# A residual attention block on one core: where the low parts of the column tiles' weights are made

## Chip, core and metric

The kernel runs on one core of a Trainium2 chip. The metric is the device time of one execution in microseconds. Three runs of the kernel before took 858.71, 859.07 and 860.24 us; their median is 859.07 us.

## What is computed

One layer on 512 tokens of width 2048, in float32: an RMS norm, one input projection that is cut into queries, keys, values and gates of eight stick-breaking heads and into the latents and gates of eight latent-attention heads, both attentions, an output projection, a second norm and the residual.

```python
h = rms_norm(x, pre_norm_w)
proj = h @ w_in
sb_q, sb_k, sb_v, sb_gate, c_q, c_kv, k_rope, mla_gate = jnp.split(proj, split_pts, axis=-1)
o_a = from_heads(stick_breaking_attention(to_heads(sb_q, SB_HEADS), to_heads(sb_k, SB_HEADS), to_heads(sb_v, SB_HEADS)))
...
o_b = from_heads(chunk_causal_softmax_attention(q_mla, k_mla, v_mla.transpose(0, 2, 1, 3)))
mixed = jnp.concatenate([o_a * jax.nn.silu(sb_gate), o_b * jax.nn.silu(mla_gate)], axis=-1)
y = mixed @ w_out
return x + rms_norm(y, post_norm_w)
```

## The kernel before

**Two parts of a number.** TensorE multiplies values of a shorter float type (float32r). Each float32 operand is therefore held as a high part, the value rounded to that type, and a low part, the value less its high part. A product of two operands is three matmuls that add up in one PSUM bank (`mm3`): high by high, high by low, low by high.

**Weights.** `weights` (line 104) brings a piece of 128 x 1024 float32, 512 KB, and splits it. SyncE's queue (SP) loads it into a `raw` tile, of which there are two. ScalarE (ACT) casts it to the high part `whi` (line 96), then VectorE (DVE) subtracts to get the low part `wlo` (line 99). There are three `whi` and three `wlo` tiles, so the parts of one piece can be made once TensorE (PE) has finished with the piece three places earlier.

```python
i = act.copy(out=hi, in_=src)
dve.tensor_tensor(out=lo, in0=src, in1=hi.bitcast(F32), op=ALU.subtract)
```

**Column tiles.** `column_proj` (line 217) makes 128 columns of the input projection, transposed, for all tokens. One column tile takes two pieces of `w_t`, and each piece serves 8 products of three 128x512 matmuls. In a product the matmul that reads `wlo` comes last. There are 32 column tiles, 64 pieces: the gates of the eight latent heads (PSUM tile `gps`), and a query (`qp`), a key (`kp`) and a gate (`gps`) tile for each stick-breaking head. The pieces of the other projections (`cq`, `ckv`, `v`) and of the output (`y`) come through `weights` as well, in the same three-tile ring.

**Order of the work.** PE runs its matmuls in the order in which the program states them. A generator (`filler`, line 449) holds everything that isn't attention: `ckv`, the latent heads' gates, then for every fourth head four heads' values, and for each head query, key and gate, and last the output projection. Attention code calls `fill(n)` to put n of these products between its own steps, so that PE has something to do while ACT and DVE work on scores. The other engines' orders come from a scheduler. Each engine runs its own list strictly in order, and an instruction that waits holds up those behind it.

**GpSimd's queue (POOL)** is touched too. It issues the loads of the latent heads' small weights (`mraw`, line 114), it clears two small tiles for each head (`th` and `tl`, lines 588 and 589), it puts each head's result `mix` aside in memory (`mixed`, line 607) and brings it back for the output projection (`mx`, line 392). A load of `mraw` waits for DVE to be done with the load before it, a store of `mix` for DVE's product, and a load of `mx` for DVE's split of an earlier one.

**Attention.** In a latent head ACT takes the exponentials `p` of the scores `mz` (line 662), after loading its table of functions. PE's next scores wait for `p` where both buffers of scores are taken. In a stick-breaking head ACT computes `keep` and `beta` (lines 745 and 746).

Of the kernel before, what the change touches and what calls it, by code (L numbers as in the profile page):

```python
# [10 lines left out]
F32 = mybir.dt.float32  # L11
F32R = mybir.dt.float32r
# [7 lines left out]
P = 128  # L20
# [12 lines left out]

# slots of [128, 512] float32 by kind, and pieces of the weights in flight
SLOTS = {"g": 46, "q4": 4, "row": 6, "tr": 4, "t": 4, "gt": 2, "mv": 4, "qrt": 8}
# [5 lines left out]
def _bits(v, n):  # L41
    """v cut to n significant bits."""
    m, e = math.frexp(v)
    return math.ldexp(float(round(math.ldexp(m, n))), e - n)
# [13 lines left out]
def block(ctx: ExitStack, tc: tile.TileContext, a: dict):  # L58
# [28 lines left out]
    def load(out, in_):  # L87
        tc.keep_in_program_order(nc.sync.dma_start(out=out, in_=in_))
# [3 lines left out]

# [1 line left out]
    def split(hi, lo, src, scale=None, pin=False):  # L94
# [9 lines left out]
    def weights(src, n):  # L104
# [5 lines left out]
        return hi, lo  # L110

    def small_weights(src, n, pin=False):
        raw = ring.tile([P, 768], F32, tag="mraw", name="mraw", bufs=1)
        pool.dma_start(out=raw[:, :n], in_=src)
        hi = ring.tile([P, 768], F32R, tag="mhi", name="mhi", bufs=1)
        lo = ring.tile([P, 768], F32R, tag="mlo", name="mlo", bufs=1)
        split(hi[:, :n], lo[:, :n], raw[:, :n], pin=pin)
        return hi, lo

    # TensorE runs what is traced, in that order: the order below keeps it fed.  # L120
    def mm(out, lhsT, rhs, start, stop, **kw):
# [9 lines left out]

# [1 line left out]
    pre_w = const.tile([P, NK], F32, name="pre_w")  # L133
# [18 lines left out]
    def rms_factor(name, ss, n, cols):  # L152
        """(ss / n + eps) ** -0.5"""
        m = tn(name + "_m", cols)
        dve.tensor_scalar(out=m, in0=ss, scalar1=1.0 / n, scalar2=EPS, op0=ALU.mult, op1=ALU.add)
        r = const.tile([P, cols], F32, name=name)
        pool.tensor_tensor(out=r, in0=m, in1=mhalf[:, :cols], op=ALU.pow)
        return r

    # TensorE's clock rises while it works  # L160
    idle = g("idle", BF16)
# [4 lines left out]

# [1 line left out]
    hh, hl = [], []  # L168
# [20 lines left out]
    def group_proj(src, width, banks, first=False):  # L189
        """Token-major projection of all blocks of tokens, chunk by chunk; yields after each product."""  # L190
        cuts = [(0, 1), (1, 2)] if first else [(0, 2)]
        cuts += [(k, k + 2) for k in range(2, NK, 2)]
        for k0, k1 in cuts:
            parts = []
            if first:
                # the first chunk of x comes in halves, the weights between them
                parts = [load_h(k, (slice(0, 256), slice(256, S)) if k == 0 else (slice(0, S),)) for k in range(k0, k1)]
                for p_ in parts:
                    next(p_)
            i, o = k0 // 2, (k0 % 2) * width  # L200
            wh, wl = weights(src[i, :, o:o + (k1 - k0) * width], (k1 - k0) * width)
            for p_ in parts:
                next(p_, None)
            for k in range(k0, k1):
                c = slice((k - k0) * width, (k - k0 + 1) * width)
                if first and k == 0:
                    for st, mv in ((hh, wh), (hl, wh), (hh, wl)):
                        for b in range(NB):
                            mm(banks[b][:, :width], tokens(st[k], b), mv[:, c], st is hh and mv is wh, False)
                    continue  # L210
                for b in range(NB):
                    mm3(banks[b][:, :width], tokens(hh[k], b), tokens(hl[k], b), wh[:, c], wl[:, c], k == 0, k == NK - 1)
                    yield
            if first and k0 >= 4:
                square_x(3)

    def column_proj(t, out):
        """One tile of 128 columns, transposed: [column, token]; yields after each product."""
        for half in range(2):
            wh, wl = weights(a["w_t"][t, half], 1024)  # L220
            for j in range(8):
                k = half * 8 + j
                c = slice(j * P, (j + 1) * P)
                mm3(out, wh[:, c], wl[:, c], hh[k], hl[k], k == 0, k == NK - 1)
                yield

# [1 line left out]
    cq_banks = [zbank("cq") for _ in range(2)] + [tbank("cq") for _ in range(2)]  # L228
    for _ in group_proj(a["w_cq"], 512, cq_banks, first=True):
        pass  # L230

# [1 line left out]
    pos_i = tiny.tile([P, NB], I32, tag="tinyi", name="pos_i", bufs=1)  # L233
# [18 lines left out]
    def turns(n, unit, name):  # L252
        """fraction of a turn in n * unit radians, n a whole number of at most 12 bits"""
        c1, c2, c3 = _parts(math.fmod(unit / TWO_PI, 1.0), (12, 12))
        t = sm(name)
        dve.tensor_scalar(out=t, in0=n, scalar1=c1, scalar2=None, op0=ALU.mult)
        w = rounded(t, 1.0, name + "w")
        dve.tensor_tensor(out=t, in0=t, in1=w, op=ALU.subtract)
        fma(t, n, c2, t)
        fma(t, n, c3, t)  # L260
        return t
# [25 lines left out]

    # [block, half, 32]: cosines twice; sines with the sign of their half; the queries' ones scaled
    tabs = {}
# [22 lines left out]
    def latent(banks, n, width, name):  # L312
        """The scaled projection, token-major, and the sums of squares of its first n columns."""
        ssl = const.tile([P, NB], F32, name=name + "ss")
        cs = []
        for b in range(NB):
            c = g(f"{name}{b}")
            dve.tensor_scalar(out=c[:, :width], in0=banks[b][:, :width], scalar1=rstd[:, b:b + 1], scalar2=None, op0=ALU.mult)
            junk = g("junk", tag="tr")
            act.activation(out=junk[:, :n], in_=c[:, :n], func=AF.Square, accum_out=ssl[:, b:b + 1])  # L320
            cs.append(c)
        return cs, ssl
# [12 lines left out]

# [1 line left out]
    done = {}  # L337

    def gate(t, name):
        """silu of a tile of gate columns, transposed."""  # L340
        ps = bank("gps")
        yield from column_proj(t, ps)
        gr = g(name, tag="gt")
        dve.tensor_tensor(out=gr, in0=ps, in1=rstd_bc, op=ALU.mult)
        sg = g("sg", tag="tr")
        act.activation(out=sg, in_=gr, func=AF.Sigmoid)
        dve.tensor_tensor(out=gr, in0=gr, in1=sg, op=ALU.mult)
        return gr
# [26 lines left out]

    # chunks of the output projection: the latent heads' first
    order = list(range(H, 2 * H)) + list(range(H))
# [43 lines left out]
    def resident_weights():  # L421
        """The next two chunks of the last columns' weights."""
        raw = ring.tile([P, 1024], F32, tag="raw", name="raw", bufs=N_RAW)
# [53 lines left out]
    def rotary_queries(grp, new_bank):  # L477
# [10 lines left out]
        ps = [new_bank("qrp") for _ in range(2)]  # L488
        # the two blocks of a bank are one accumulation, which the first of its products starts
        for c in range(4):  # L490
# [23 lines left out]
    def rotary_turn(stacks):  # L514
        """[high; low] of four heads' rotary queries, transposed."""
        out = []
# [9 lines left out]

# [1 line left out]
    cqs, ssq = latent(cq_banks, 512, 512, "cq")  # L528
# [13 lines left out]

    # rstd of every token along the free axis, on every partition
    rb_ps = zbank("rb_ps")
# [8 lines left out]

# [1 line left out]
    ct, st = tabs["k"]  # L555
# [13 lines left out]

# [1 line left out]
    def row_tiles(name):  # L571
        """The rows of the four blocks of queries, the short ones beside each other."""
        t0, t1, t2 = (g(name, tag="row") for _ in range(3))
        return [t0[:, 384:], t1[:, :256], t0[:, :384], t2]

    class Weighted:
        """(sum over s of vals[s, :]^T rows[q, s]) * gate, transposed, by blocks of keys."""

# [29 lines left out]

# [1 line left out]
    def mla_values(pair):  # L610
# [13 lines left out]
    class Latent:  # L624
        """Scores and softmax of a latent head."""

# [58 lines left out]
    for h in range(H + 1):  # L685
# [39 lines left out]
        if h < H and h % 2 == 0:  # L725
            fill(2)
            vals[h // 2] = mla_values(h // 2)
            fill(2)
        # a head's worth of gate columns for every head
        fill(max(0, 4 * NK + NK * (h + 2) - taken[0]))  # L730

# [1 line left out]
    for h in range(H):  # L733
# [27 lines left out]

# [1 line left out]
    for _ in steps:  # L763
# [94 lines left out]
```

## Time and profile before

| what | value |
|---|---|
| median of three runs | 859.07 us (858.71 to 860.24) |
| profiled execution, first to last instruction (span) | 857.2 us |
| own time of the profiled execution | not recorded beside its span; the median is 1.9 us above the span |
| PE busy | 844.1 us, 98% of the span |
| DVE busy | 425.0 us, 50% |
| ACT busy | 337.8 us, 39% |
| POOL busy | 42.1 us, 5% |
| bytes moved by DMA | 97.19 MB, a mean of 113 GB/s |

The busy time of an engine is the sum of its instructions. Matmuls are pipelined and their ends are modelled, so one is shown as 389 ns long while the next starts 227 ns after it. The chain of waits follows the span back from its last instruction, at each step to what released it. PE is named on 93% of it.

### The profile page before, as it was taken

To read this page: it belongs to the slowest core of one execution; us is meant where nothing else is said; L and a number is where in the kernel's file an instruction comes from. 1 tells how busy PE (TensorE), PEld (TensorE's weight loads), DVE (VectorE), ACT (ScalarE), POOL (GpSimd) and SP (SyncE) were. 2 spreads that over 40 slices of the span, in tenths; PEclk is the share of its full clock that TensorE was granted. 3 is DMA by queue.
4 is the path that set the end of the run, shared out by engine and by line. 5 is a ranking of instruction groups with operands and counts; after the bars stand their busy time and mean duration, and the time that the engine had idled before them with its cause. 6 is when DMAs were issued, how large, how long until landed. Compare 5 with 4: busy or idle time off the path is not lost.

```text
span 857.2 us, 10780 instructions
## 1 busy us (share of the span) xinstructions
PE 844.1 (98%) x4146; PEld 711.9 (83%) x4146; DVE 425.0 (50%) x757; ACT 337.8 (39%) x585; POOL 42.1 (5%) x100
## 2 busy tenths in 40 slices
PE   8999999999999999999999999999999999999995
PEld 5889988888888888888888888888888888888885
DVE  5576755556556433536354524446364623244333
ACT  6743655554454423424243314323243423134201
POOL 1010000000000110000000000000001000000001
PEclk9999999999999999999999999999999999999998
DMA  9823222222221252222222224222223232336364
GB/s 314 317 75 101 99 86 75 81 93 80 93 81 62 76 192 97 79 100 85 97 88 86 89 96 135 99 86 95 89 81 132 97 110 99 111 103 204 112 190 153
DMA packets 32627, 97.19 MB, mean 113 GB/s; under 512 B 4144, under 2 KB 4672, under 8 KB 32576
## 3 DMA queue, kind: packets, MB, share of 16 engines
q1 hardware_dynamic: 27792, 82.46, 28.5%
q0 software_dynamic: 3488, 12.08, 4.3%
q10 hardware_dynamic: 1296, 1.97, 0.7%
q8 instruction: 32, 0.52, 0.3%
q14 instruction: 19, 0.16, 0.1%
HBM read 88.37 MB, written 8.13 MB: 113 GB/s over the span
## 4 chain that ended last, share of the span: by engine, by line
PE 93%; DVE 3%; ACT 1%; DMA 1%; issue 0%; POOL 0%; DVEq 0%; SPq 0%; ACTq 0%; POOLq 0%
PE y L122 20%; PE gps L122 19%; PE qp L122 10%; PE v L122 10%; PE kp L122 10%; PE cq L122 4%; PE av L122 4%; PE mz L122 3%; PE mqp L122 3%; PE ckv L122 2%; PE tp L125 2%; PE z L122 2%; PE qrp L122 1%; PE mv L122 1%; PE mkp L122 1%; DMA raw<-in_w_cq 1%
## 5 line engine op out<-in xcount | busy, mean ns | idle before, releaser
L99 DVE TENSOR_TENSOR wlo<-raw,whi 128x1024 fp32r<-128x1024 f32 (+2 forms) x124 | 147.5, 1190 | 187.8 <-ACT whi L96 186.0
L96 ACT CAST whi<-raw 128x1024 fp32r<-128x1024 f32 (+2 forms) x124 | 127.0, 1024 | 251.5 <-PE y L122 58.4
L122 PE MATMUL gps<-hh,whi 128*128 128x512 f32 x256 | 102.0, 398 | 0.0
L122 PE MATMUL gps<-hl,whi 128*128 128x512 f32 x256 | 100.1, 391 | 0.0
L122 PE MATMUL gps<-hh,wlo 128*128 128x512 f32 x256 | 99.9, 390 | 0.0
L122 PE MATMUL y<-whi,mxh 128*128 128x512 f32 (+1 forms) x222 | 85.5, 385 | 0.0
L122 PE MATMUL y<-whi,mxl 128*128 128x512 f32 (+1 forms) x222 | 85.1, 383 | 0.0
L122 PE MATMUL y<-wlo,mxh 128*128 128x512 f32 (+1 forms) x222 | 85.1, 383 | 0.0
L122 PEld LDWEIGHTS gps<-hh,wlo 128*128 128x128 f32 x256 | 48.1, 188 | 10.6
L122 PEld LDWEIGHTS gps<-hl,whi 128*128 128x128 f32 x256 | 48.2, 188 | 7.6
L122 PEld LDWEIGHTS gps<-hh,whi 128*128 128x128 f32 x256 | 48.2, 188 | 7.5
L122 PE MATMUL qp<-hh,whi 128*128 128x512 f32 x128 | 52.0, 407 | 0.0
L96 ACT CAST th<-tp 128x512 fp32r<-128x512 f32 (+1 forms) x64 | 27.1, 423 | 63.2 <-PE tp L125 63.2
L99 DVE TENSOR_TENSOR tl<-tp,th 128x512 fp32r<-128x512 f32 (+1 forms) x64 | 31.2, 488 | 39.9 <-ACT th L96 39.5
L122 PE MATMUL v<-whi,hh 128*128 128x512 f32 x128 | 50.9, 397 | 0.0
L122 PE MATMUL qp<-hh,wlo 128*128 128x512 f32 x128 | 50.1, 391 | 0.0
L122 PE MATMUL qp<-hl,whi 128*128 128x512 f32 x128 | 50.0, 391 | 0.0
L122 PE MATMUL v<-whi,hl 128*128 128x512 f32 x128 | 49.9, 390 | 0.0
L122 PE MATMUL v<-wlo,hh 128*128 128x512 f32 x128 | 49.9, 390 | 0.0
L122 PE MATMUL kp<-hh,whi 128*128 128x512 f32 x128 | 49.8, 389 | 0.0
L122 PE MATMUL kp<-hl,whi 128*128 128x512 f32 x128 | 49.8, 389 | 0.0
L122 PE MATMUL kp<-hh,wlo 128*128 128x512 f32 x128 | 49.8, 389 | 0.0
(246 smaller groups left out, 1618.5 us busy)
## 6 DMA issues: line engine op xcount, KB each, us to landing
raw<-in_w_t SPq DMA_DIRECT2D x64, 512.0 KB, 3.2
raw<-in_w_o SPq DMA_DIRECT2D x32, 512.0 KB, 3.2
raw<-in_w_v SPq DMA_DIRECT2D x16, 512.0 KB, 3.2
xs<-in_x SPq DMA_DIRECT2D x16, 256.0 KB, 6.2
xr<-in_x SPq DMA_DIRECT2D x16, 256.0 KB, 4.9
xt<-in_xt SPq DMA_DIRECT2D x15, 256.0 KB, 5.7
mixed<-mix POOLq DMA_DIRECT2D x15, 256.0 KB, 2.3
mx<-mixed POOLq DMA_DIRECT2D x15, 256.0 KB, 3.4
```

What stands on the lines that cost most here:

```text
L96: i = act.copy(out=hi, in_=src)
L99: dve.tensor_tensor(out=lo, in0=src, in1=hi.bitcast(F32), op=ALU.subtract)
L122: tc.keep_in_program_order(pe.matmul(out=out, lhsT=lhsT, rhs=rhs, start=start, stop=stop, **kw))
L125: tc.keep_in_program_order(pe.transpose(out, in_, identity))
```

## The change

`column_proj` takes its pieces from a new function. ACT now writes the negated high part into `wlo`: it multiplies by -1 and rounds to float32r in one instruction. A DMA on POOL's queue then reads the same piece of the weights from memory a second time and adds it onto `wlo` in place. ACT makes `whi` with a second instruction. DVE no longer takes part in these 64 pieces. All other pieces go through `weights` as before.

```diff
+    def weights_by_dma(src, n):
+
+        raw = ring.tile([P, 1024], F32, tag="raw", name="raw", bufs=N_RAW)
+        load(out=raw[:, :n], in_=src)
+        hi = ring.tile([P, 1024], F32R, tag="whi", name="whi", bufs=N_HI)
+        lo = ring.tile([P, 1024], F32R, tag="wlo", name="wlo", bufs=N_HI)
+        act.activation(out=lo[:, :n], in_=raw[:, :n], func=AF.Copy, scale=-1.0)
+        pool.dma_start(out=lo[:, :n], in_=src, accum_op=ALU.add)
+        act.copy(out=hi[:, :n], in_=raw[:, :n])
+        return hi, lo
+
...
     def column_proj(t, out):
...
         for half in range(2):
-            wh, wl = weights(a["w_t"][t, half], 1024)
+            wh, wl = weights_by_dma(a["w_t"][t, half], 1024)
             for j in range(8):
```

The orders of PE and of SP stay as they were. Those of ACT, DVE and POOL are the scheduler's, and they change at many places. In the kernel of the change line numbers are 11 higher from `small_weights` on; line 118 is the negation, 119 the accumulating DMA and 120 the cast.

The first place is ACT in the first latent head, between the split of its keys (`mkh`) and its exponentials (`p`). Before:

```order
91 L96 CAST mkh<-mkp 128x512
92 L96 CAST whi<-raw 128x1024
93 L346 ACT_TABLE_LOAD
94 L346 ACTIVATE sg<-mg 128x512
95 L662 ACT_TABLE_LOAD
96 L662 ACTIVATE p,sm<-mz,nm 128x128
```

And now:

```order
96 L96 CAST mkh<-mkp 128x512
97 L120 CAST whi<-raw 128x1024
98 L118 ACTIVATE wlo<-raw 128x1024
99 L357 ACT_TABLE_LOAD
100 L357 ACTIVATE sg<-mg 128x512
101 L673 ACT_TABLE_LOAD
102 L673 ACTIVATE p,sm<-mz,nm 128x128
```

One instruction, the negation, stands in front of the gate's sigmoid `sg` and of the first exponential.

The second place is ACT where the fifth stick-breaking head begins, around the split of its queries (`qh`). Before:

```order
324 L96 CAST mxh_5969<-mx 128x512
325 L96 CAST mxh_6005<-mx 128x512
326 L96 CAST whi<-raw 128x1024 x2
327 L96 CAST qh<-qp 128x512
328 L96 CAST whi<-raw 128x1024 x2
```

And now:

```order
376 L96 CAST mxh_6033<-mx 128x512
377 L96 CAST mxh_6069<-mx 128x512
378 L120 CAST whi<-raw 128x1024
379 L118 ACTIVATE wlo<-raw 128x1024
380 L120 CAST whi<-raw 128x1024
381 L96 CAST qh<-qp 128x512
382 L118 ACTIVATE wlo<-raw 128x1024
383 L120 CAST whi<-raw 128x1024
384 L118 ACTIVATE wlo<-raw 128x1024
```

Each cast has a negation behind it, and one of the negations stands behind the split of the queries too.

The third place is POOL from the end of the fourth stick-breaking head to the end of the fifth. Before:

```order
72 L588 MEMSET th 128x128
73 L589 MEMSET tl 128x128
74 L607 DMA mixed_1217<-mix 128x512
75 L392 DMA mx<-mixed_1214 128x512
76 L392 DMA mx<-mixed_1215 128x512
77 L392 DMA mx<-mixed_1216 128x512
78 L588 MEMSET th 128x128
79 L589 MEMSET tl 128x128
80 L607 DMA mixed_1218<-mix 128x512
```

And now:

```order
90 L599 MEMSET th 128x128
91 L600 MEMSET tl 128x128
92 L618 DMA mixed_1218<-mix 128x512
93 L119 DMA wlo<-in_w_t 128x1024 x3
94 L403 DMA mx<-mixed_1215 128x512
95 L403 DMA mx<-mixed_1216 128x512
96 L403 DMA mx<-mixed_1217 128x512
97 L119 DMA wlo<-in_w_t 128x1024 x7
98 L599 MEMSET th 128x128
99 L600 MEMSET tl 128x128
100 L618 DMA mixed_1219<-mix 128x512
```

Ten accumulating DMAs have come between POOL's own work, three of them ahead of the loads of `mx` and seven behind them.

## Rows read from the trace of the kernel before

**Rows 1.** The page: busy time by engine, and the chain of waits by engine.
```profile
PE 844.1 (98%) x4146; PEld 711.9 (83%) x4146; DVE 425.0 (50%) x757; ACT 337.8 (39%) x585; POOL 42.1 (5%) x100
...
PE 93%; DVE 3%; ACT 1%; DMA 1%; issue 0%; POOL 0%; DVEq 0%; SPq 0%; ACTq 0%; POOLq 0%
```

**Rows 2.** Busy us by stretch: length, PE, PEld, DVE, ACT, POOL; clock, DMA, GB/s.
```profile
98.00:270.00 172.00, 171.31 (x897) 146.34 (x896) 104.25 (x243) 91.02 (x177) 13.00 (x30) 1.00 0.24 81
270.00:522.00 252.00, 252.00 (x1179) 210.19 (x1178) 114.72 (x170) 87.80 (x134) 10.06 (x26) 1.00 0.29 99
522.00:670.00 148.00, 148.00 (x692) 123.66 (x691) 78.14 (x117) 56.63 (x93) 6.70 (x16) 1.00 0.31 104
```

**Rows 3.** Waits of PE: for whom, us in total, times, longest.
```profile
PE cq L122 <- DVE wlo L99: 1.0, 2, 0.8
PE mz L122 <- ACT p L662: 0.7, 1, 0.7
...
PE av L122 <- DVE tl L99: 0.2, 1, 0.2
```

**Rows 4.** Groups by shape: count, busy us, mean ns, idle before and its releasers.
```profile
L99 DVE TENSOR_TENSOR wlo<-raw,whi 128x1024 fp32r<-128x1024 f32 x114 | 139.6, 1224 | 181.4 <-ACT whi L96 179.6 <-PE av L122 1.1
```

**Rows 5.** Timeline of ACT, the second place of the change: start, length, instruction.
```profile
532.72 1.05 ACT L96 CAST whi<-raw 128x1024 fp32r<-128x1024 f32 x1 [4.38 <-PE qp L122]
533.67 0.58 ACT L96 CAST qh<-qp 128x512 fp32r<-128x512 f32 x1
```

**Rows 6.** Timeline of PE: first matmul on `wlo` of two pieces.
```profile
533.20 0.39 PE L122 MATMUL kp<-hh,wlo 128*128 128x512 f32 x1
...
544.08 0.39 PE L122 MATMUL gps<-hh,wlo 128*128 128x512 f32 x1
```

**Rows 7.** Timeline of ACT at the casts of the first two column pieces.
```profile
88.78 1.05 ACT L96 CAST whi<-raw 128x1024 fp32r<-128x1024 f32 x1
...
93.02 1.05 ACT L96 CAST whi<-raw 128x1024 fp32r<-128x1024 f32 x1 [0.36 <-PE ckv L122]
93.97 1.17 ACT L522 CAST qrt<-qtp 128x512 fp32r<-128x512 f32 x2
```

**Rows 8.** Timeline of PE: first matmul on the first column piece's `wlo`.
```profile
98.41 0.39 PE L122 MATMUL gps<-hh,wlo 128*128 128x512 f32 x1
```

**Rows 9.** DMA issues: KB each, median us from issue to landing.
```profile
raw<-in_w_t SPq DMA_DIRECT2D x64, 512.0 KB, 3.2
...
mraw<-in_w_head POOLq DMA_DIRECT2D x8, 384.0 KB, 3.3
...
mraw<-in_w_kvv POOLq DMA_DIRECT2D x4, 256.0 KB, 2.8
```

**Rows 10.** DMA queue of SP: packets, MB, share of 16 engines' span.
```profile
q1 hardware_dynamic: 27792, 82.46, 28.5%
```

**Rows 11.** Timeline of ACT and PE, the first place of the change.
```profile
114.54 1.05 ACT L96 CAST whi<-raw 128x1024 fp32r<-128x1024 f32 x1 [2.29 <-PE gps L122]
...
118.85 0.37 ACT L662 ACTIVATE p<-mz,nm 128x128 f32<-128x128 f32 x1
...
119.36 0.44 PE L122 MATMUL mz<-mkh,mqh 128*128 128x384 f32 x1 [0.69 <-ACT p L662]
```

**Rows 12.** Timeline of POOL at four places.
```profile
112.78 0.55 POOL L114 DMA_DIRECT2D mraw<-in_w_head  x1 [5.72 <-DVE mlo L99]
132.46 0.55 POOL L114 DMA_DIRECT2D mraw<-in_w_head  x1 [19.13 <-DVE mlo L99]
...
451.93 0.54 POOL L607 DMA_DIRECT2D mixed<-mix  x1 [5.88 <-DVE mix L603]
...
525.93 1.75 POOL L392 DMA_DIRECT2D mx<-mixed  x3 [35.69 <-DVE mxl L99]
```

**Rows 13.** Busy us in one stick-breaking head, columns as in rows 2.
```profile
365.20:403.00 37.80, 37.80 (x179) 31.60 (x178) 18.59 (x28) 13.15 (x21) 0.95 (x3) 1.00 0.27 91
```

## Prediction

> **What bounds the kernel now.** I began with the page. PE is busy for 844.1 of 857.2 us and is named on 93% of the chain, while DVE is busy for half of the span, ACT for 39% and POOL for 5% [rows 1]. So an instruction that leaves DVE is worth only what PE waits for it. Column tiles run from 98 to 670 us, and the table of stretches gives PE 171.31 of 172 us, 252 of 252 and 148 of 148, at a granted clock of 1.00 (the 2.4 GHz level) [rows 2]. All that could be won there is 0.69 us. PE's waits say what it is: 0.7 us for the exponentials `p` of ACT, once, and 0.2 us for `tl`. The 1.0 us that PE waits for a `wlo` belongs to the tile `cq`, at the start, which the change leaves alone [rows 3]. DVE does stand idle for 179.6 us until a cast ends [rows 4], but nobody on the path waits for DVE. The question is therefore not what DVE gains, but whether the new way of making `wlo` stays inside the time that the old one had to spare.
>
> **DVE's part.** Removed are 64 subtractions of 1.224 us [rows 4], 78 us of DVE's 425. Their cover is PE's work, so I count 0. At most they give back 0.69 us, all the idle time that there is.
>
> **ACT's part.** Added are 64 negations. The nearest row is the cast of the same shape, 1.05 us [rows 5]: 67 us, which lifts ACT from 338 to about 405 of 857 us, so the engine doesn't become the bound. What counts is who stands behind a negation. In the first latent head it lies between the cast at 114.54 and the exponential at 118.85, for which PE already waits 0.69 us, until 119.36 [rows 11]. There is no cover left, so the whole delay goes to the end. An instruction behind such a cast starts 0.95 us after it (93.02 to 93.97 [rows 7]), so this costs **+0.95 us**. Elsewhere PE waits for no work of ACT between 98 and 670 us, and I take 0. The other end is 0.95 us in each of the seven other latent heads, 6.7 us.
>
> **SP's part.** SP's list is the same. A `raw` tile used to be free 1.05 + 1.22 us after its cast began, when the subtraction ended; now it is free after two ACT instructions, 0.95 + 1.05 us. The loads come no later: 0.
>
> **POOL's part.** Added are 64 issues of about 0.55 us [rows 12], 35 us on an engine with 42 busy. They queue in order with waiting instructions. Where the fifth stick-breaking head begins, three loads of `mx` wait until 525.93 and take 1.75 us, so POOL is free at 527.7 [rows 12]. The fourth accumulation stands behind them. The casts come one piece apart, 5.44 us (PE's first `wlo` matmuls at 533.20 and 544.08 are two pieces apart [rows 6]), so its cast begins at about 532.72 - 5.44 = 527.28 [rows 5], its negation ends 2.0 us later, and it finds POOL free with 1.6 us to spare. After a head's store of `mix` (0.54 us at 451.93) POOL is free at once. I count 0, and a hold counts like a longer landing (first rival).
>
> **The accumulation itself.** This operation isn't in the trace, so I set its landing against the time that it has. That time is shortest at the second place of the change. There the cast starts at 532.72, the split `qh` ends at 534.25 [rows 5], the negation would end at about 535.2, and PE wants this `wlo` at 544.08 [rows 6]: **8.9 us**. The first column piece is a second tight spot: its cast ends at 89.83 [rows 7] and PE reads its `wlo` at 98.41 [rows 8], 8.6 us, or 7.6 us if the negation stands behind the cast.
>
> The landing can't be shorter than that of a plain load. POOL's loads land after 2.8 us for 256 KB and 3.3 us for 384 KB [rows 9], so 512 KB need about 3.8 us: the low end. How much is data? SP's queue spent 28.5% of 857.2 us on 82.46 MB [rows 10], 2.96 us for a MB, so a piece of 0.524 MB keeps all engines busy for 1.55 us. An accumulation also has to read its destination. If this doubles the data's part, it lands after 3.8 + 1.55 = **5.4 us**. The high end is reading the weights, reading the destination and writing it one after another, each as long as a load: 3 x 3.8 = 11.4 us. I take 5.4 us, since the row nearest to it is POOL's load, with the same issue and the same bytes from memory. This is under 7.6 us, so it costs 0.
>
> The Trainium skill has a rule on the doubling (Collectives: The Full Stack, "The bandwidth ceiling: the fold count and why AG ≠ RS ≠ AR"): the add in the DMA engine costs nothing by itself, but the two reads halve an engine's rate, from about 31 to 16 GB/s. By that, an estimate, 32 KB on each of 16 engines take 2.0 us where the rows give 3.1, and the sum stays as it is. No row here shows an accumulation.
>
> POOL's loads, with DVE busy half the time, land about as fast as SP's 512 KB in 3.2 us [rows 9], so I see no hindrance of POOL's transfers by DVE. The Trainium skill names one that speaks against this change (SBUF — State Buffer, "A bandwidth-pool intuition that's wrong"): a transfer issued by POOL took about 3.1 in place of 0.62 us beside a DVE copy, because its descriptors had to wait. By that rule the landing would be about 5.4 + 2.5 = 7.9 us, an estimate, still inside 8.9 us but not always inside the first piece's 7.6, and the sum would be 0 to 0.3 us higher.
>
> **Traffic.** For each piece the DMA engines would be busy 1.55 us for the load and 3.1 us for the accumulation, 4.65 us. A piece is due every 5.44 us at the densest and every 37.8 / 6 = 6.3 us over a stick-breaking head [rows 13]. It fits.
>
> **Sum.** 857.2 + 0.95 = 858.2 us for the span. The median of the runs stands 1.9 us above this execution's span, so I forecast **860.0 us**, 0.1% more. A measurement of this kernel can tell about 0.2% (1.7 us) from no change; this would mostly be read as the same.
>
> **Rivals.**
> 1. *A wait of PE on the accumulation* (slower). Place: the third matmul of a product on a new piece, at the first column piece and once in each of the eight stick-breaking heads, where the room is smallest. It decides from a landing, holds on POOL included, of some 7.6 us at the first and 8.9 us at the others. From there each further us costs about 9 us in all. At the high end, 11.4 us, it is 3.8 + 8 x 2.5 = 24 us: 884. For it: nothing in the trace bounds the read of the destination, and POOL's queue holds for up to 19.13 us in the latent heads [rows 12]. Against it: 5.4 us leaves more than 2 us.
> 2. *The DMA engines become the bound* (much slower). This decides where the accumulation keeps them busy for over 6.3 - 1.55 = 4.75 us a piece, three times a plain load. At six times, 9.3 us, 48 pieces lack 10.85 - 6.3 = 4.55 us each, 218 us: 1078. Against it: DMA is busy 24 to 31% in these stretches [rows 2], and double reading adds only 3.1 us to a piece.
> 3. *ACT's extra instruction is paid in every latent head* (slower): 6.7 us more, 866.7. Against it: a single wait for `p` in the trace.
> 4. *Faster*: the lists of ACT and DVE fall so that the one wait doesn't grow and the 0.69 us go: 856.5 for the span, 858.4, still within 0.2%. More than that PE hasn't got to give in these stretches.
>
> **How the numbers follow.** The forecast has a chance of 0.60, rival 1 0.20, rival 2 0.10, rival 3 0.08, rival 4 0.02. Of the forecast 0.52 lies within 0.2%, 0.07 above (some more ACT delays) and 0.01 below. Of rival 1, 0.18 is over 0.2% slower and 0.02 within; rival 2 is slower; rival 3 gives 0.07 slower and 0.01 within; rival 4 splits evenly. Together: faster 0.02, same 0.56, slower 0.42. The range runs from rival 4's 858.4, less 0.2 for the spread of the runs, to rival 1 at its high end, 884, and 1 us for the term of ACT's bound: 858.2 to 885. It leaves out rival 2 and some of the edges.
>
> **What would show it.** In the profile after: a DMA row `wlo<-in_w_t` x64 with a median landing of some 5 to 6 us; DVE near 347 us and ACT near 405 us busy; PE's wait for `p` up from 0.7 to about 1.6 us; no wait of PE for `wlo` between 98 and 670 us. Landings over 9 us with PE waiting on `wlo` in each head are rival 1, a DMA share near 1 there is rival 2, seven waits for `p` are rival 3. I am wrong if PE loses more than 2 us between 98 and 670 us.

## The result, and the profile after

The changed kernel takes **864.43 us** (863.61 to 864.50), the kernel before 859.07: 1.0058 times as long, interval 1.0038 to 1.0078. That is 5.4 us more. It lies inside the range, but it is not the 860.0 of the forecast, and it is not within the 0.2% that the prediction calls the same.

The page of the kernel after, busy time and chain, stands against [rows 1]:

```profile
PE 845.3 (98%) x4146; PEld 712.7 (83%) x4146; DVE 351.9 (41%) x693; ACT 395.7 (46%) x649; POOL 96.0 (11%) x164
...
PE 87%; issue 3%; DMA 3%; ACT 2%; DVE 2%; POOL 1%; DVEq 0%; SPq 0%; ACTq 0%; POOLq 0%
```

DVE lost 73 us and ACT gained 58; the forecast was 78 and 67. What is new is that DMA, ACT, DVE and "issue" hold 10% of the chain; before it was 5%. The stretches, with the columns of [rows 2], tell where:

```profile
98.00:270.00 172.00, 169.17 (x879) 143.78 (x878) 86.90 (x226) 101.98 (x190) 25.18 (x44) 1.00 0.52 129
270.00:522.00 252.00, 252.00 (x1184) 210.40 (x1183) 84.83 (x144) 110.89 (x159) 31.46 (x52) 1.00 0.62 148
522.00:670.00 148.00, 148.00 (x691) 123.63 (x691) 51.26 (x90) 76.43 (x112) 25.96 (x39) 1.00 0.81 185
```

The latent heads, 98 to 270 us, lose 2.1 us of PE's busy time against [rows 2]. The stick-breaking heads lose nothing, though the DMA engines are 2.1 to 2.6 times as busy as before, and the granted clock is 1.00 everywhere. PE's waits, against [rows 3], name two waits that grew, and neither is for `wlo`:

```profile
PE mz L133 <- ACT p L673: 1.6, 1, 1.6
PE av L133 <- DVE tl L99: 1.5, 3, 0.7
```

PE executes the same 4146 matmuls in the same order in both traces, so the start of each can be subtracted from its start before. The shift is 0.15 us at 98 us. It jumps by 0.95 us at the matmul of [rows 11] (119.36 before, now 120.47), by 0.74 us at two near 189 us, by 1.24 us at three near 235 us and by 0.32 us between 672 and 675 us. At the last matmul it is 3.46 us. The span grew by 5.6 us (862.8 for 857.2), so 2.1 us more are lost *after* the last matmul. There the work is the same; what differs is the last DRAIN of POOL and of SP. The source view of the program's last line, before and then after; the columns are shortest, median and longest ns, then the first and last start in us:

```profile
L854 POOLq DRAIN  x3: 40/102/5619, 850.5 to 856.9; - x3
L854 SPq DRAIN  x3: 7/7/7, 856.4 to 856.7; - x3
```

```profile
L865 POOLq DRAIN  x3: 46/102/7982, 854.0 to 862.5; - x3
L865 SPq DRAIN  x3: 7/7/7, 859.8 to 862.2; - x3
```

POOL's longest drain started at 850.55 and took 5.62 us: done at 856.2, just under SP's first drain at 856.4. Now it starts at 854.0, takes 7.98 us and ends at 862.0, when SP has been ready since 859.9. These are the 2.1 us.

The DMA issues and the queues of the kernel after, against [rows 9, 10]:

```profile
raw<-in_w_t SPq DMA_DIRECT2D x64, 512.0 KB, 4.4
wlo<-in_w_t POOLq DMA_DIRECT2D x64, 512.0 KB, 7.7
```

```profile
q1 hardware_dynamic: 27792, 82.46, 29.7%
q0 software_dynamic: 12704, 45.64, 26.8%
```

An accumulation lands after 7.7 us, not 5.4, and SP's loads beside it became slower (4.4 for 3.2 us). PE still never waits for one: over all tiles from 98 us on the longest landing is 8.5 us.

Where do the shifts at 189 and 235 us come from? The chain of waits of the kernel after, in order of time (start, us, what), at the first of them:

```profile
181.19 0.54 POOL wlo L119
181.73 7.00 DMA mraw<-in_w_head
188.72 0.02 issue
188.75 0.02 ACTq L96
188.76 0.04 issue
188.80 0.84 ACT mhi L96
189.65 0.02 issue
189.67 0.41 DVE mlo L99
190.08 0.47 issue
190.55 0.56 DVE tl L99
191.11 0.04 issue
191.15 0.62 PE av L133 x2
```

Read it upwards. PE waits for `tl`; DVE made it late because `mlo` stood ahead of it; `mlo` waited for ACT's `mhi`; and `mhi` waited for the small weights `mraw`, whose load POOL issued right behind an accumulation. The load took 7.0 us. Its median before was 3.3 [rows 9]. Nobody needs these small weights yet, but ACT and DVE work in order, and the rows of the softmax queue behind them.

The 0.3 us between 672 and 675 us have a cause of the same kind. The chain there starts with the first of four loads of `mx`, which POOL issues next after its last accumulation. It lands after 4.1 us; in the kernel before it landed after 2.9. This was read off the traces and not tried by itself.

### The profile page after: what moved, and what is told of

Its sections match the earlier page's. It is cut to its first block, busy times and chain, and to the rows that moved or that the text cites. A ratio compares the mean times of both kernels' runs of the same rounds, so it can differ in the third digit from the quotient of the medians.

```text
span 862.8 us, 10897 instructions
## 1 busy us (share of the span) xinstructions
PE 845.3 (98%) x4146; PEld 712.7 (83%) x4146; DVE 351.9 (41%) x693; ACT 395.7 (46%) x649; POOL 96.0 (11%) x164
## 4 chain that ended last, share of the span: by engine, by line
PE 87%; issue 3%; DMA 3%; ACT 2%; DVE 2%; POOL 1%; DVEq 0%; SPq 0%; ACTq 0%; POOLq 0%
PE y L133 20%; PE gps L133 16%; PE qp L133 10%; PE v L133 10%; PE kp L133 10%; PE cq L133 4%; PE av L133 3%; PE mz L133 2%; PE ckv L133 2%; PE mqp L133 2%; PE tp L136 2%; DMA mraw<-in_w_head 2%; PE z L133 2%; PE qrp L133 1%; DMA raw<-in_w_cq 1%
## 5 line engine op out<-in xcount | busy, mean ns | idle before, releaser
L96 ACT CAST whi<-raw 128x1024 fp32r<-128x1024 f32 (+2 forms) x60 | 59.6, 993 | 129.7 <-PE y L133 57.1
L99 DVE TENSOR_TENSOR wlo<-raw,whi 128x1024 fp32r<-128x1024 f32 (+2 forms) x60 | 69.2, 1154 | 105.7 <-ACT whi L96 105.5
L120 ACT CAST whi<-raw 128x1024 fp32r<-128x1024 f32 x64 | 67.1, 1048 | 88.1 <-issue 38.9
L119 POOL DMA_DIRECT2D wlo<-in_w_t x64 | 54.7, 854 | 342.5 <-ACT wlo L118 292.1
L118 ACT ACTIVATE wlo<-raw 128x1024 fp32r<-128x1024 f32 x64 | 67.6, 1056 | 15.3 <-PE v L133 14.9
```

The lines of the kernel that those rows point to most:

```text
L118: act.activation(out=lo[:, :n], in_=raw[:, :n], func=AF.Copy, scale=-1.0)
L119: pool.dma_start(out=lo[:, :n], in_=src, accum_op=ALU.add)
L120: act.copy(out=hi[:, :n], in_=raw[:, :n])
```

## The experiments

My theory after this reading had **three costs**: the negation ahead of the first softmax (1.0 us), small weights that land late behind accumulations (2.0 us at two heads; the expectations below say 1.9), and POOL's longer last drain (2.1 us). The rivals were ScalarE's 67 us as such, and DMA traffic as such. In the table, "98 to last" is the shift gathered between 98 us and the last matmul. The shift before 98 us is left out there because the first loads land differently from one execution to the next: two runs below with the same list of first loads differ by 2.1 us at 20 us. "Tail" is the time from the last matmul to the end of the span, less the 9.2 us of the kernel before. Ratios are to the kernel before beside which each ran.

| run | median us | ratio (95%) | 98 to last | tail | POOL's longest drain, us | DMAs that POOL issued |
|---|---|---|---|---|---|---|
| the change | 864.43 | 1.0058 (1.0038 to 1.0078) | +3.3 | +2.1 | 7.98 | 110 |
| e4 stick-breaking heads only | 860.01 | 1.0017 (1.0008 to 1.0026) | +0.7 | +0.7 | 6.59 | 94 |
| e8 gates of latent heads only | 862.82 | 1.0048 (1.0034 to 1.0062) | +3.0 | +1.4 | 6.92 | 62 |
| e1 addition on VectorE | 864.40 | 1.0069 (1.0057 to 1.0082) | +5.3 | 0.0 | 5.62 | 46 |
| e6 negation on VectorE | 861.31 | 1.0027 (1.0018 to 1.0036) | 0.0 | +2.1 | 7.98 | 110 |
| e2 plain load | 864.57 | 1.0068 (1.0051 to 1.0085) | +1.1 | +5.0 | 10.84 | 110 |
| e7 two halves | 862.98 | 1.0051 (1.0036 to 1.0066) | +3.8 | +0.8 | 6.68 | 174 |
| e3 two buffers for mraw | 864.21 | 1.0067 (1.0054 to 1.0079) | +1.2 | +2.1 | 7.98 | 110 |
| e3 mraw on SP | 861.94 | one run | +0.1 | +1.3 | 7.20 | 98 |
| e9 mraw on SP but the first | 859.96 | 1.0012 (1.0003 to 1.0021) | -0.2 | +1.4 | 7.25 | 99 |
| e9 the same, negation on VectorE | 860.67 | 1.0021 (1.0013 to 1.0029) | -0.2 | +1.4 | 7.25 | 99 |
| e10 before, mraw on SP | 858.91 | 0.9995 (0.9986 to 1.0003) | +0.4 | -0.2 | 4.72 | 35 |
| e5 64 small DMAs | 904.62 | one run | not used | +5.0 | 10.85 | 110 |

**Which part of the program pays.** Accumulation for some tiles only:

```diff
-            wh, wl = weights_by_dma(a["w_t"][t, half], 1024)
+            wh, wl = (weights_by_dma if t < 24 else weights)(a["w_t"][t, half], 1024)
```

(`t < 24` are the 48 pieces of the stick-breaking heads; the other run has `t >= 24`, the 16 pieces of the latent heads' gates.)

> Accumulation for the 48 pieces of the stick-breaking heads only; the 16 pieces of the latent heads' gates are made by VectorE's subtraction as before. My theory: nothing is lost up to the last matmul (no wait at 119, 191 or 237 us), and GpSimd's last drain grows with the number of DMAs that GpSimd issues (46 before, 110 in the change, 94 here: 37 ns each, 7.4 us): 1.5 us at the end, 860.6 us. Rival (the drain does not go by the number of DMAs but is there or not): 861.2. Rival (contention wherever accumulations run, in proportion): 863.1.

> Accumulation for the 16 pieces of the latent heads' gates only. My theory: the waits at 119, 191 and 237 us stay (+3.5 us by the last matmul, less the 0.3 us at 675 us), the drain is 5.62 + 16 x 0.037 = 6.2 us, of which 0.3 us shows: 862.6 us. Rival (contention in proportion, 16 of 64 pieces): 860.4. Rival (drain there or not): 864.4.

Both came out near the first theory, and far from "in proportion": 16 of the 64 accumulations cost 4.1 us (862.82 against 858.73), the other 48 cost 1.3. What the theory had wrong is the drain. It is 6.92 us with 62 DMAs and 6.59 with 94, so 37 ns for each can't be the law.

**ScalarE's part alone.** The addition stays on VectorE, nothing accumulates:

```diff
-        pool.dma_start(out=lo[:, :n], in_=src, accum_op=ALU.add)
+        dve.tensor_tensor(out=lo[:, :n], in0=raw[:, :n], in1=lo[:, :n].bitcast(F32), op=ALU.add)
```

> ScalarE still writes the negated high parts ahead of the cast, VectorE adds the raw weights to them (64 additions, like the 64 subtractions of the kernel before); no accumulating DMA. My theory has three costs in the change: ScalarE's negation ahead of the first latent head's softmax (+1.0 us), the small weights' loads late behind accumulations on GpSimd's queue (+1.9 us at two latent heads, +0.3 to +0.5 besides), and a longer last drain of GpSimd (7.98 us for 5.62, +2.1 us of it at the end). It expects only the first here: 860.1 us, PE's longest wait for the softmax 1.6 us, drain 5.6 us, last load of mraw ahead of TensorE's need. Rival ScalarE (its 67 us of extra work make all the loss): 864.4. Rival DMA (all the loss comes from the accumulations and their traffic): 859.1.

A miss of 4.3 us, and an instructive one. The jump at 119 us came (0.96 us), the drain was 5.62 us, the waits at 189 and 235 us were gone. But six of the eight stick-breaking heads lost 0.4 to 0.7 us at their first score, and 0.2 us more in small steps behind it. DVE and then ACT of this run, where such a head begins:

```profile
352.08 1.23 DVE L119 TENSOR_TENSOR wlo<-raw,wlo 128x1024 fp32r<-128x1024 f32 x1 [1.17 <-ACT wlo L118]
353.23 0.68 DVE L99 TENSOR_TENSOR kl<-kr,kh 128x512 fp32r<-128x512 f32 x1
```

```profile
351.00 1.05 ACT L118 ACTIVATE wlo<-raw 128x1024 fp32r<-128x1024 f32 x1
351.96 0.60 ACT L96 CAST kh<-kr 128x512 fp32r<-128x512 f32 x1
```

The negation holds `kh` back on ACT, and VectorE's addition, which starts only when the negation ends, holds `kl` back behind it. In the change the same place reads, ACT first:

```profile
353.07 1.05 ACT L118 ACTIVATE wlo<-raw 128x1024 fp32r<-128x1024 f32 x1
354.03 0.60 ACT L96 CAST kh<-kr 128x512 fp32r<-128x512 f32 x1
```

```profile
354.67 0.69 DVE L99 TENSOR_TENSOR kl<-kr,kh 128x512 fp32r<-128x512 f32 x1 [1.67 <-ACT kh L96]
```

`kl` follows `kh` at once. So ScalarE's negation is not free in the stick-breaking heads; it is paid for there by the VectorE instruction that is gone. The median equals that of the change by accident: other microseconds.

**The negation on VectorE**, the accumulation as in the change:

```diff
-        act.activation(out=lo[:, :n], in_=raw[:, :n], func=AF.Copy, scale=-1.0)
+        dve.tensor_scalar(out=lo[:, :n], in0=raw[:, :n], scalar1=-1.0, scalar2=None, op0=ALU.mult)
```

> The changed kernel with the negated high parts written by VectorE (64 multiplications by -1), not ScalarE; the DMA accumulates onto them as in the change. My theory: the wait at 119 us falls from 1.6 back to 0.7 us, since ScalarE has nothing more ahead of the first latent head's softmax than in the kernel before; in the stick-breaking heads VectorE's negation stands where its subtraction stood, at no cost; the late small weights (+1.9 us) and the last drain (7.98 us) stay: 863.4 us. Rival (the wait at 119 us is a VectorE or DMA matter): 864.4, wait still 1.6.

It went to 861.31: the wait at 119 us fell to 0.7 us as expected, and the 2.0 us of the small weights went too, which I had not expected. The last matmul stands where it stood in the kernel before (0.04 us earlier), and all that is left is the drain's 2.1 us. POOL's timeline, here first and then in the change, says why:

```profile
180.26 0.56 POOL L125 DMA_DIRECT2D mraw<-in_w_head  x1 [7.34 <-DVE mlo L99]
181.10 0.89 POOL L119 DMA_DIRECT2D wlo<-in_w_t  x1 [0.28 <-issue]
```

```profile
181.19 0.85 POOL L119 DMA_DIRECT2D wlo<-in_w_t  x1 [7.11 <-ACT wlo L118]
181.73 0.88 POOL L125 DMA_DIRECT2D mraw<-in_w_head  x1
```

With the negation moved, the order on POOL's queue came out the other way round: the load is issued 0.8 us ahead of the accumulation, not 0.5 us behind it. ACT reads it at 184.85, 4.6 us after its issue, in place of 7.1.

**Accumulating or only loading.** The same 64 DMAs, plain, so that the subtraction is left out:

```diff
-        pool.dma_start(out=lo[:, :n], in_=src, accum_op=ALU.add)
+        pool.dma_start(out=lo[:, :n], in_=src.bitcast(F32R) if hasattr(src,'bitcast') else src)
```

> The changed kernel with the 64 DMAs on GpSimd's queue as plain loads over the negated high parts, not accumulating; so the low part becomes the whole weight, and the subtraction is left out. Order, waits and bytes are those of the change. My theory: the accumulation itself is what makes the landing long (7.7 us, and about 3.0 us of all 16 DMA engines for each piece against 1.55 for a plain one, by the queue's busy share), so a plain load lands in 4 to 5 us, the small weights behind it land in about 4 us, and the waits at 191 and 237 us shrink below 0.3 us; the wait at 119 us and the last drain (same number of DMAs) stay: 862.3 us. Rival (the queue and the bytes make the landing long, not the accumulation): landing 7 us, waits as they were, 864.4.

```profile
L119 POOL DMA_DIRECT2D wlo<-in_w_t x64 | 34.1, 532 | 354.8 <-ACT wlo L118 308.6
...
wlo<-in_w_t POOLq DMA_DIRECT2D x64, 512.0 KB, 4.6
```

```profile
q0 software_dynamic: 12704, 45.64, 15.5%
```

On TensorE it went as expected: landing 4.6 us, the small weights behind such a load in 4.9 us, no wait at 189 or 235 us; the 1.0 us at 119 us stayed. A plain issue holds POOL for 0.53 us, an accumulating one for 0.85. From q0's shares, less the kernel before's 36.9 us (4.3% of 857.2), a plain piece keeps all 16 DMA engines busy for 1.5 us and an accumulated one for 3.0. The drain, though, is 10.84 us, not the 7.98 that I expected, and takes back all of the gain.

**The small weights out of the way**, in four runs. A second buffer:

```diff
-SLOTS = {... "row": 6 ...}
+SLOTS = {... "row": 5 ...}
-        raw = ring.tile([P, 768], F32, tag="mraw", name="mraw", bufs=1)
+        raw = ring.tile([P, 768], F32, tag="mraw", name="mraw", bufs=2)
```

> The changed kernel with two buffers in place of one for the raw small weights (and five slots of the kind row in place of six, to make room). My theory: the load of the small weights is issued one piece of small weights earlier, so that neither its hold on GpSimd's queue nor its landing of 7 us reaches the softmax rows of the latent heads; PE's waits of 0.6 to 0.9 us for tl near 191 and 237 us vanish, the 1.0 us at 119 us and the drain stay: 862.5 us. Rival (the waits there come from ScalarE's or VectorE's later order, not from the load): 864.4, waits as they were. Rival DMA contention: 864.4.

All of them on SP's queue:

```diff
-        pool.dma_start(out=raw[:, :n], in_=src)
+        nc.sync.dma_start(out=raw[:, :n], in_=src)
```

> The changed kernel with the small weights loaded by SP's queue, not GpSimd's. If the long landing of the small weights (7.0 us at 181 and 228 us, 3.6 in the middle) comes from standing behind an accumulation in the same queue, it is 3 to 4 us here, and the waits at 191 and 237 us go unless SP holds the load back behind a load of raw that waits for its buffer: 862.5 us. If it comes from the DMA engines, which all queues share, it stays 5 to 7 us. The last drain tells more of what it goes by: 98 DMAs on GpSimd's queue, all 64 accumulations.

With both, the jumps at 189 and 235 us are gone (at most 0.2 us is left), while ScalarE still makes the 64 negations. With two buffers the accumulations stand where they stood, and the loads behind those at 184 and 230 us still land late (5.3 and 6.8 us for 256 KB); only no reader waits for them yet. So it is the late load. The two-buffer run's median didn't fall. Its profile lost 3.0 us before 98 us; how much of that is the missing `row` slot and how much the spread of the first loads was not tried apart.

On SP's queue the longest landing of `mraw` between 175 and 240 us was 5.1 us (7.5 in the change). But the scheduler had moved the accumulations too, and none was in flight beside that load, so this run alone doesn't tell the place in the queue from a share of the DMA engines. Loads of one size in two of the runs come closer to it. With the small weights on SP's queue and the negation on VectorE (below), a 256 KB load of `mraw` issued 0.4 us behind an accumulation on POOL's queue landed after 3.2 us at 189 us and 3.4 us at 233 us. In the two-buffer run, on POOL's own queue and 0.9 and 0.6 us behind, it took the 5.3 and 6.8 us. Most of the delay therefore comes with the place in the queue. Not all of it need do so: three such loads on SP's queue near 141 us, about 2 us behind an accumulation, took 4.5 to 5.4 us.

The wait at 119 us went as well on SP's queue: the scheduler put cast and negation behind the softmax row, not ahead of it.

Then with the first of the small weights left on POOL's queue, in the change, in the change with the negation on VectorE, and in the kernel before:

```diff
-        pool.dma_start(out=raw[:, :n], in_=src)
+        (pool if pin else nc.sync).dma_start(out=raw[:, :n], in_=src)
```

> The changed kernel with the small weights on SP's queue, but for the first of them, which stays on GpSimd's, so that the first loads of x keep their place. My theory: the 1.6 us that the run with all of them on SP lost before 16 us is not lost; the waits at 191 and 237 us are gone (under 0.3 us); the wait at 119 us is 1.6 or, as in that run, gone; the last drain is about 7.2 us: 860.7 to 861.7 us.

> Both edits: negation on VectorE, small weights but the first on SP's queue. If the change's loss is the three costs of my theory and nothing else, only the last drain (7.2 us for 5.62, of which 1.3 shows) and 0.3 us near 675 us are left: 860.6 us. If 861.5 or more, there is a fourth cost. If it is below 858.5, freeing VectorE is worth something after all.

> The kernel before (VectorE's subtraction, no accumulation) with the small weights but the first on SP's queue. In its order ScalarE's cast of the raw weights stands behind the first softmax row of the first latent head, not ahead of it. My theory: the wait of 0.7 us at 119 us goes, nothing else moves before the last matmul; the last drain, by 81.4 ns for each of GpSimd's DMAs (35 for 46), is 4.7 us and hidden behind SP's last waits: 0.8 to 1.0 us less than the kernel before, 858.1. Against the change with the same edit it then measures what the accumulations cost where the small weights are out of their way: about 1.9 us, 1.4 of it the drain. Rival (the run with the small weights on SP was short because VectorE was free): 859.1 here.

With the small weights off POOL's queue the change loses nothing on balance between 98 us and the last matmul, with the negation on either engine: PE gains 0.96 us at 119 us, where the wait of the kernel before went too, and gives 0.7 us back in small steps, 0.3 of it between 672 and 675 us. The first e9 run came 0.7 us below the lowest that was expected, by that gain. The second came on its number, 2.0 us of early loads in its profile aside; but that number didn't count the gain. So there is no fourth cost of a microsecond, while some tenths could hide behind the gain.

The last run was to beat both kernels and doesn't; its time is nearer to the 859.1 of its rival. PE's wait at 119 us went (0.96 us), but 1.3 us came back in small steps between 141 and 637 us, half of it near 189 us, and 0.9995 is no difference. There a small load was late without any accumulation: issued at 180.85 us on SP's queue, 0.4 us ahead of two loads of `raw`, it took 5.8 us. No run here beats the kernel before. The last run is still useful beside e9. With equal queues, accumulation takes 859.96 against 858.91 (0.8 us over the kernel before beside which it ran, against 0.1), and the traces give 1.6 us to the longer tail and 0.6 us *back* on PE from 98 us on. That half a microsecond may be what freeing VectorE is worth (argued, not shown); the drain eats it.

**What the drain goes by.** 64 DMAs of 4 bytes a partition added to the kernel before, and each accumulation in two halves:

```diff
             wh, wl = weights(a["w_t"][t, half], 1024)
+            pool.dma_start(out=tiny.tile([P, 1], F32, tag="dummy", name="dummy", bufs=1), in_=a["w_t"][t, half][:, :1])
```

> The kernel before with 64 more DMAs on GpSimd's queue, each of 4 bytes a partition into a tile that nothing reads, one after each piece of the column tiles' weights; VectorE's subtractions stay. It asks what the last drain of GpSimd goes by. If by the number of DMAs alone (110 as in the change): 7.98 us for 5.62 and 861 us. If by accumulations or bytes: 5.62 us and 859. TensorE's waits as in the kernel before up to 0.5 us.

```diff
-        pool.dma_start(out=lo[:, :n], in_=src, accum_op=ALU.add)
+        for c in (slice(0, n // 2), slice(n // 2, n)):
+            pool.dma_start(out=lo[:, c], in_=src[:, c], accum_op=ALU.add)
```

> Each accumulation in two of half the columns: 128 issues for 64, the same bytes. My theory: each issue holds GpSimd 0.85 us, the small weights behind come 0.5 us later, and each of the two waits (191, 237 us) grows by up to 0.5 us; the first wait stays: about 865.4 us. On the last drain: if it goes by the descriptors written since some point, it moves (5 to 8 us); if by the bytes, 7.98. Rival (accumulations are off the path but for their traffic): 864.4, nothing moves.

The small DMAs shared one tile, so each waited for the one before on POOL's queue and held up the small computations there; PE waited 30.2 us at `ckv`, and that run's time says nothing. Its drain does: 10.85 us, like the 64 plain loads of 512 KB (10.84), so it doesn't go by bytes. All 64 were issued by 182 us and still count at the end. The longest drain of e10, e8, e2 and e5, in that order, as the third of the three durations:

```profile
L854 POOLq DRAIN  x3: 40/102/4721, 852.4 to 858.6; - x3
...
L865 POOLq DRAIN  x3: 46/102/6921, 852.9 to 860.3; - x3
...
L865 POOLq DRAIN  x3: 46/102/10842, 851.3 to 862.6; - x3
...
L855 POOLq DRAIN  x3: 40/102/10846, 891.3 to 902.6; - x3
```

With 35, 46, 62 and 110 DMAs it is 4.72, 5.62, 6.92 and 10.84 us: **81.6 ns for each DMA that GpSimd issued**, whatever its size; the 16 accumulations of e8 are on that line. With 48 and more accumulations it is shorter than the line says (7.98 for 110, 7.25 for 99, 6.59 for 94, 6.68 for 174 with the halves), as if some DMAs no longer counted: by the line, 33 to 36 are missing in each of these runs, and 115 with the halves. Why, no run told, and it stays open. The halves were also a miss in time. PE lost a little more than in the change (3.8 us), as expected, but the shorter drain gave more back.

## Why the range held and the forecast did not

The forecast had the direction right, +0.95 us, and the size wrong: +5.4 us. That 864.43 lies between 858.2 and 885 is luck. The upper part of the range was there for PE waiting on the accumulation itself, and neither that nor seven more waits on ACT came. Two terms were taken as nothing, what stands behind an accumulation on POOL's queue and the end of the program. They make 4.1 of the 5.6 us between the two profiles.

- **ACT's term held.** +0.95 us at [rows 11] was forecast and 0.95 measured; the run with the addition on VectorE has it without any DMA. "Elsewhere 0" also held, but its reason was incomplete. I took it from PE's not waiting for ACT. e1 shows that 4.3 us would be paid in the stick-breaking heads if the subtraction ahead of `kl` had not gone at the same time. The other end of that term put the cost into the seven other latent heads, the wrong place.
- **DVE's term held:** 73 us less busy, nothing gained on the path. The bound beside it, 0.69 us for all that PE could win, was too low. Where the wait at 119 us went altogether (e9, e10), PE gained 0.96 us, since a matmul is shown as 389 ns long while the next one can start after 227 ns.
- **POOL's term failed, by 2.0 us.** I counted what a waiting POOL does to the accumulations, "a hold counts like a longer landing", and checked that against `wlo` alone. What stands *behind* an accumulation in the same queue I did not price: the next load of `mraw` [rows 12]. In the kernel before one was issued at 180.32 us and read by ACT at 184.29: 4.0 us, for a load that takes 3.3 [rows 9]. That had next to no room, and the trace shows it. An issue was mis-sized as well, 0.85 us for the 0.55 of a plain one. Rival 1 has the mechanism (POOL's queue in order, a landing too long) but the wrong victim.
- **The landing was mis-sized:** 5.4 us forecast, 7.7 measured, within the bounds of 3.8 and 11.4. The plain load from POOL lands after 4.6 us, not 3.8, and accumulating adds 3.1 us, not 1.55. PE's room for `wlo` was still enough, as argued. The price fell on the load behind.
- **No term for the end of the program: 2.1 us.** The sum was "span plus waits" and took the tail as fixed. In the kernel before POOL's drain lay 0.3 us under SP's last waits; 64 more DMAs bring it out. No row that I read showed it. The source view of the last line shows how little room there was, though not that the drain goes by the number of DMAs.
- **Traffic held.** 3.0 us of all engines for an accumulation against 3.1 forecast; the densest stretch is 81% busy and PE loses nothing in it.

The sum, from the two profiles: 1.0 (first softmax) + 2.0 (small weights) + 0.3 (`mx`, near 675 us) + 0.2 (small shifts and the 0.15 us before 98 us) + 2.1 (drain) = 5.6 us, the difference of the spans. My own mark, "wrong if PE loses more than 2 us between 98 and 670 us", was passed with 3.0 us of shift.

The two rules weighed before: the add costs an engine half of its rate because both operands are read (the Trainium skill, Collectives: The Full Stack, "The bandwidth ceiling: the fold count and why AG ≠ RS ≠ AR", where it is said of the reduce step of a collective). The runs agree on the doubling, 1.5 to 3.0 us of engine time, though not on the 2.0 us that was estimated from the page's rates. The other was that POOL's transfers wait for their descriptors beside VectorE's copies (the Trainium skill, SBUF — State Buffer, "A bandwidth-pool intuition that's wrong (but worth ruling out)"). From it I had an estimated landing of 7.9 us, and 7.7 was measured, but that agreement is luck: with VectorE just as busy (351.8 us) the plain load from the same queue lands after 4.6 us.

## What to carry to other kernels

A DMA put on a queue is paid by what stands behind it there: before moving work onto GpSimd's queue, list the loads that follow it, with the time that each has before its reader, and ask which instructions queue behind that reader on the in-order engines. An instruction added ahead of a cast on one engine can be hidden by one removed ahead of the next step on another, so the two sides of a swap have to be tried together and apart. And the end of a program is not a constant: read the last drains before adding DMAs to GpSimd, since those that it issues are counted there.

## What the runs showed of the hardware that I had not expected

- GpSimd's last drain lasts 81.6 ns longer for every DMA that it issued, from 4.72 us at 35 to 10.84 us at 110, the same for 512 KB and for 4 bytes a partition; with 48 or more accumulating DMAs it falls below that line (7.98 us at 110).
- An accumulating DMA of 512 KB holds GpSimd for 0.85 us at issue (plain 0.53), lands after 7.7 us (plain 4.6) and keeps the DMA engines busy for 3.0 us (plain 1.5).
- A 384 KB load issued 0.5 us behind such a DMA on the same queue took 7.0 and 7.5 us, behind a plain one 4.9 and 4.3, and 0.8 us ahead of one 4.5.
